# Host layouts for the streams, output and weights of a two-layer diffusion block, and first modulations taken chunk by chunk

## The chip, the cores and the metric

The kernel runs on one core of one Trainium2 chip. The metric is the device time of one execution in microseconds (us), median of several runs. A profiled execution gives the trace. TensorE is called PE in the rows, its weight loads PEld, VectorE DVE, ScalarE ACT, GpSimd POOL, and SyncE's issue of transfers SPq.

## The reference

Two consecutive layers work on 256 latent tokens (x) and 256 context tokens (ctx), each of width 1024, in float32. Each layer is a half-step feed-forward block, a mixing block, and a second half-step feed-forward block; each is modulated by shift, scale and gate vectors that a matrix w_mod makes from a conditioning vector:

```python
def rms_norm(x, gain=None):
    y = xf * lax.rsqrt(jnp.mean(xf * xf, axis=-1, keepdims=True) + EPS)
...
def modulate(h, shift, scale):
    return h * (1.0 + scale) + shift

def swiglu(h, w_gate, w_up, w_down):
    return (jax.nn.silu(h @ w_gate) * (h @ w_up)) @ w_down
```

The mixing of the even layer is windowed attention beside differential attention, that of the odd layer latent attention beside neighbourhood attention. Nine modulation vectors a layer are silu(c) @ w_mod + b_mod, once for the latent tokens (from c) and once for the context tokens (from c_ctx). Only the latent tokens are returned.

## The kernel before

**Layout.** The stream lies transposed in SBUF as `xT`: eight chunks k of 128 features by 512 tokens (latent 0 to 255, context 256 to 511). A weight block of 512 KB (four k-chunks of 128 rows by 256 columns) is loaded by `wcols` (L269) into one of three buffers `raw`; in a (1024, 2816) matrix that is 512 pieces of 1 KB. `split` then writes two reduced-precision halves into `hs`: high on ACT (L99), low on DVE (L100). Each product is three matmuls, high by high, high by low, low by high, in `mm3` (L103).

**A feed-forward block.** For each pair of 128-column groups, `gps0, gps1` (gate) and `ups0, ups1` (up) are summed over the eight chunks of `hT`, the modulated and normed stream; then ACT makes silu (`sg`, L428), DVE the product (`af`), both are split (`ah`), and later `dps` (down) goes back into `xT` (L295).

**The start.** The tokens are loaded as they come, 128 tokens by 1024 features (`xin`, L505). ACT squares and sums them (L549); PE transposes them in 32 pieces (`xps`, L555), and ACT and DVE copy these into `xT`. c, c_ctx and b_mod are loaded as rows and transposed too (`cps`, `bps`). The first feed-forward block needs shift and scale of layer 0, 1024 values each for two streams, from 8 MB of w_mod: in four quarters q of two chunks each. `first_loads(q)` issues four loads of 512 KB (`wm`, L515), `first_mods(q)` runs 32 small matmuls into `mps` (L524; each is two records in the trace), copies it (`mst`, L527), transposes (`mpt`, L529) and adds the bias (L96), and `first_norm(q)` makes `xn` (L540) and `hT` (high L542, low L543). For the first pair of the first block the product is interleaved with the quarters: as soon as chunks 0 and 1 of `hT` are there, their 24 matmuls can run.

**The other modulations** are not matmuls: rows of the transposed w_mod (`mraw`, L202, 512 KB each) are multiplied by `cb` (c and c_ctx broadcast to all partitions, L199, silu in place at L200) and summed by one DVE instruction for each (L212). This stream of parts is called between the matmuls (`pump_every`), from the first pair on.

**The end.** The last block computes the latent tokens alone. For each of the eight chunks of the result `emit_out` transposes two halves (`otp`, L488), copies them into `ot` (L491 on ACT, L493 on DVE), and writes 128 by 256 values after every second chunk (L496).

**Order.** A scheduler of the language places every instruction in its engine's list before the run; each engine then works through its own list in order, and semaphores join the lists. All large transfers are issued by SP, in order. A transfer waits at SP for its buffer to be free and for the semaphore of the transfer that stood eight places earlier; those behind it wait with it.

Of the kernel before, what the change touches and what calls it, by code (L numbers as in the profile page):

```python
# [16 lines left out]
P = 128  # L17
# [23 lines left out]
UNITS = {"kq": 15, "ot": 6, "pr": 9, "pt": 10, "w2": 8, "wm": 16, "xn": 4, "hT": 8, "raw": 3, "hs": 5, "mraw": 3}  # L41
# [22 lines left out]
def tile_hybrid_dit(ctx: ExitStack, tc: tile.TileContext, I, out, dbg=None):  # L64
# [101 lines left out]
    bT = const("bT", [P, 2, 9, KC])  # L166
    brow = w2("brow")[:72, :256]
    Q.dma_start(out=brow.rearrange("n (l p) -> n l p", l=2), in_=I["b_mod"].rearrange("l (n p) -> n l p", p=P))

    S.activation(cvec, cvec, AF.Silu)  # L170
    cps = bank("tr", "cps")
    T.transpose(cps[:, :16], cvec, ident[:16, :16])
    for v in range(2):
        V.tensor_copy(cT[:, :, v], cps[:, 8 * v:8 * v + 8])
    bps = bank("tr", "bps")
    for l in range(2):
        T.transpose(bps[:, 72 * l:72 * l + 72], brow[:, l * P:(l + 1) * P], ident[:72, :72])
    V.tensor_copy(bT, bps[:, :144].rearrange("p (l m k) -> p l m k", l=2, m=9))
# [86 lines left out]
    def wcols(w, k0, nk, c0, nw, tag=None):  # L265
        n = nk * nw
        src = w[k0 * P:(k0 + nk) * P, c0:c0 + nw].rearrange("(k p) f -> p k f", p=P)
# [14 lines left out]
    xall = xp.tile([P, KC, NTOK], F32, tag="xT", name="xT")  # L282
    xT = [xall[:, k, :] for k in range(KC)]
# [197 lines left out]
    outs = {}  # L481

    def emit_out(dc):
        if dc % 4 == 0:
            outs["t"] = [w2(f"ot{b}") for b in range(2)]
        for b in range(2):
            pt = bank("tr", "otp")
            T.transpose(pt[:, :P], xT[dc][:, b * P:(b + 1) * P], ident)  # L488
            o = outs["t"][b][:, (dc % 4) * P:(dc % 4 + 1) * P]
            if b:  # L490
                S.copy(o, pt[:, :P])  # L491
            else:
                V.tensor_copy(o, pt[:, :P])  # L493
            if dc % 2 == 1:
                c0 = (dc % 4 - 1) * P
                Q.dma_start(out=out[b * P:(b + 1) * P, (dc - 1) * P:(dc + 1) * P],  # L496
                            in_=outs["t"][b][:, c0:c0 + 256])


    ss0 = const("ss0", [P, 4])  # L500
    xin = []
    for tb in range(4):
        t = up.tile([P, D], F32, tag="kq", name=f"xin{tb}", bufs=UNITS["kq"])
        src = I["x"][0] if tb < 2 else I["ctx"][0]
        Q.dma_start(out=t, in_=src[(tb % 2) * P:(tb % 2 + 1) * P, :])  # L505
        xin.append(t)


    def first_loads(q):
        tiles = {}  # L510
        for k0 in (0, 4):
            for m in (1, 0):
                t = up.tile([P, 4, 256], F32, tag="wm", name="wm", bufs=UNITS["wm"])
                c0 = m * D + 256 * q
                Q.dma_start(out=t, in_=I["w_mod"][0, k0 * P:(k0 + 4) * P, c0:c0 + 256].rearrange("(k p) f -> p k f", p=P))  # L515
                tiles[m, k0] = t
        return tiles

    def first_mods(q, tiles):
        ps = bank(("po", "md")[q % 2], "mps")  # L520
        for k in range(KC):
            for c in range(4):
# [8 lines left out]
        for m in (1, 0):  # L531
            for v in range(2):
                add(modT[:, 0, v, m, 2 * q:2 * q + 2], pv[:, 1 - m, :, v], bT[:, 0, m, 2 * q:2 * q + 2])
# [33 lines left out]
    def first_step(q):  # L567
# [3 lines left out]
        if q == 3:  # L571
            mod_done.update({(0, 1), (0, 0)})
# [769 lines left out]
```

## Time and profile before

| | us |
|---|---|
| median of 3 runs | 1815.4 (1815.14 to 1818.62) |
| the profiled execution, its time | 1815.71 |
| its span, first to last instruction | 1813.6 |
| PE busy | 1762.3 (97%) |
| DVE busy | 1220.6 (67%) |
| ACT busy | 738.8 (41%) |
| moved by transfers | 256.90 MB, mean 142 GB/s |

The span is what the rows below are set in; 2.1 us lie around it. A busy share of PE near the whole means that time can be won only where PE stands idle, runs slowly or does work that can go.

### The profile page before, as it was taken

The page shows a single profiled execution, that of the slowest core. Times are in us where ns is not written, and L with a number is a line of the kernel's source. Part 1 is how long each engine was busy: PE and PEld are TensorE (multiplying, and loading weights), DVE is VectorE, ACT ScalarE, POOL GpSimd, SP SyncE. Part 2 cuts the span into 40 slices and gives each one's busy share as a digit, 9 for nine tenths or more (in the row PEclk, how much of TensorE's full clock was granted, in tenths as well). Part 3 has the DMA queues.
Part 4 walks back from the last instruction along what each step waited for, and adds up shares of the span by engine and source line. Part 5 has one row for each costly group of instructions (what it writes and reads, how often), then busy time and mean ns, then how long its engine had stood idle before and what let it go on. Part 6 is the DMA issues. An engine that isn't in the chain of part 4 may idle for free.

```text
span 1813.6 us, 26777 instructions
## 1 busy us (share of the span) xinstructions
PE 1762.3 (97%) x10563; PEld 1537.5 (85%) x10563; DVE 1220.6 (67%) x2343; ACT 738.8 (41%) x1322; POOL 46.0 (3%) x25
## 2 busy tenths in 40 slices
PE   7999999999999989999999999999999998999999
PEld 5788888898998888888888988888889986789998
DVE  5999953467688699989854633333346787876664
ACT  4333132345666543222233332222334656664442
POOL 0000000011010000000000000000001011000000
PEclk9999999999999989999999999999999999999999
DMA  9777752322110237778863233233233442155552
GB/s 305 273 245 225 236 190 88 116 73 68 50 60 14 59 121 240 241 229 261 300 199 105 81 94 94 92 105 103 88 111 101 89 102 57 47 178 183 175 186 82
DMA packets 214025, 256.90 MB, mean 142 GB/s; under 512 B 21484, under 2 KB 195724, under 8 KB 213900
## 3 DMA queue, kind: packets, MB, share of 16 engines
q1 hardware_dynamic: 213900, 255.19, 45.6%
q8 instruction: 83, 1.36, 0.3%
q14 instruction: 42, 0.34, 0.1%
HBM read 254.11 MB, written 1.05 MB: 141 GB/s over the span
## 4 chain that ended last, share of the span: by engine, by line
PE 87%; DVE 7%; ACT 3%; DMA 2%; issue 1%; SPq 0%; DVEq 0%; ACTq 0%
PE ups L103 23%; PE gps L103 23%; PE dps L103 23%; PE ops L103 3%; PE po L756 2%; PE sc L103 2%; DVE hs L100 1%; DMA bias<-in_d_rpb_dram 1%; PE trp L659 1%; PE pbk L103 1%; PE pbv L103 1%; PE paq L103 1%; PE pbq L103 1%; PE ptl L724 1%; PE mps L524 1%
## 5 line engine op out<-in xcount | busy, mean ns | idle before, releaser
L100 DVE TENSOR_TENSOR hs<-raw,hs 128x1024 fp32r<-128x1024 f32 (+2 forms) x308 | 367.9, 1200 | 284.1 <-ACT hs L99 283.4
L99 ACT ACTIVATE hs<-raw 128x1024 fp32r<-128x1024 f32 (+2 forms) x308 | 314.9, 1030 | 541.4 <-PE dps L103 177.8
L103 PE MATMUL dps<-ah,hs 128*128 128x512 f32 (+1 forms) x2256 | 401.0, 338 | 0.2 <-DVE hs L100 0.2
L103 PEld LDWEIGHTS dps<-ah,hs 128*128 128x128 f32 x2256 | 350.6, 190 | 46.4 <-DVE hs L100 0.4
L103 PE MATMUL gps<-hT,hs 128*128 128x512 f32 (+1 forms) x1680 | 375.3, 380 | 4.9 <-ACT hT L542 2.7
L103 PE MATMUL ups<-hT,hs 128*128 128x512 f32 (+1 forms) x1680 | 371.6, 377 | 0.0
L103 PEld LDWEIGHTS gps<-hT,hs 128*128 128x128 f32 x1680 | 305.0, 190 | 65.5 <-ACT hT L542 3.5
L103 PEld LDWEIGHTS ups<-hT,hs 128*128 128x128 f32 x1680 | 303.3, 188 | 58.8 <-issue 1.0
L212 DVE CUSTOM_DVE_ANT_0 junk<-mraw,cb,const 128x1024 f32<-128x1024 f32 x224 | 283.6, 1283 | 16.3 <-DMA mraw<-in_k_w_modT_dram 11.1
L99 ACT ACTIVATE ah<-af 128x512 fp32r<-128x512 f32 (+1 forms) x88 | 50.4, 574 | 127.5 <-DVE af L93 93.9
L295 DVE SCALAR_TENSOR_TENSOR xT<-dps,const,xT 128x256 f32<-128x256 f32 x112 | 50.3, 480 | 77.0 <-PE dps L103 76.9
L276 POOL TENSOR_TENSOR hs<-raw,hs 128x1024 fp32r<-128x1024 f32 (+2 forms) x21 | 45.8, 2186 | 1558.2 <-ACT hs L275 1493.8
L93 DVE TENSOR_TENSOR af<-sg,ups 128x512 f32<-128x512 f32 x66 | 45.2, 685 | 41.0 <-PE ups L103 40.9
L103 PE MATMUL gps<-hTl,hs 128*128 128x258 f32 x528 | 66.8, 284 | 1.6 <-DVE hTl L373 1.0
L428 ACT ACTIVATE sg<-gps 128x512 f32<-128x512 f32 x66 | 38.9, 589 | 70.2 <-PE gps L103 70.2
L103 PEld LDWEIGHTS gps<-hTl,hs 128*128 128x128 f32 x528 | 64.7, 190 | 2.5 <-DVE hTl L373 1.2
L103 PE MATMUL ups<-hTl,hs 128*128 128x258 f32 x528 | 65.5, 283 | 0.0
L103 PEld LDWEIGHTS ups<-hTl,hs 128*128 128x128 f32 x528 | 64.4, 190 | 0.0
L100 DVE TENSOR_TENSOR ah<-af,ah 128x512 fp32r<-128x512 f32 (+1 forms) x88 | 54.6, 621 | 13.2 <-ACT ah L99 13.2
L684 DVE TENSOR_REDUCE nm<-sc 128x1 f32<-128x512 f32 (+1 forms) x80 | 53.8, 682 | 5.0 <-PE sc L103 4.6
L690 ACT ACTIVATE pr<-sc,nm 128x512 f32<-128x512 f32 (+1 forms) x64 | 40.3, 634 | 13.7 <-DVE nm L684 13.4
L304 ACT ACTIVATE sq<-xT 128x256 f32<-128x256 f32 (+1 forms) x54 | 23.6, 449 | 50.9 <-DVE xT L295 50.6
(296 smaller groups left out, 1894.3 us busy)
## 6 DMA issues: line engine op xcount, KB each, us to landing
mraw<-in_k_w_modT_dram SPq DMA_DIRECT2D x128, 512.0 KB, 4.6
raw<-in_ffn_w_gate_dram SPq DMA_DIRECT2D x88, 512.0 KB, 4.7
raw<-in_ffn_w_up_dram SPq DMA_DIRECT2D x88, 512.0 KB, 4.5
raw<-in_ffn_w_down_dram SPq DMA_DIRECT2D x80, 512.0 KB, 4.1
raw<-in_cd_w_in_dram SPq DMA_DIRECT2D x18, 512.0 KB, 3.8
wm<-in_w_mod_dram SPq DMA_DIRECT2D x16, 512.0 KB, 8.7
raw<-in_ab_w_in_dram SPq DMA_DIRECT2D x16, 512.0 KB, 3.8
raw<-in_ffn_w_down_dram SPq DMA_DIRECT2D x16, 256.0 KB, 2.7
```

Of the source, the lines that this page charges most:

```text
L93: V.tensor_tensor(out=out_, in0=a, in1=b, op=ALU.mult)
L99: S.activation(h, src, AF.Copy)
L100: V.tensor_tensor(out=l, in0=src, in1=h.bitcast(F32), op=ALU.subtract)
L103: T.matmul(ps, a, b, start=start, stop=stop)
L212: V.tensor_tensor_reduce(out=junk, in0=raw, in1=mod_c[v], scale=0.5 if m in (2, 8) else 1.0, scalar=bT[:, l, m, k:k + 1], op0=ALU.mult, op ...
L276: nc.gpsimd.tensor_tensor(out=hs[:, 1, :n], in0=raw[:, :n], in1=hs[:, 0, :n].bitcast(F32), op=ALU.subtract)
L295: V.scalar_tensor_tensor(out=xT[dc][:, a:e], in0=ps[:, a:e], scalar=modT[:, l, v, m, dc:dc + 1], in1=xT[dc][:, a:e], op0=ALU.mult, op1=ALU ...
L304: S.activation(sq[:, cols], xT[dc][:, cols], AF.Square)
L428: S.activation(sg, g[:, :ntok], AF.Silu)
L684: V.tensor_reduce(out=nm[:, c], in_=view, axis=AX.X, op=ALU.max, negate=True)
L690: S.activation(p[:, cols], sc[:, cols], AF.Exp, bias=nm[:, i + b:i + b + 1], accum_out=den[:, i + b:i + b + 1])
L756: T.matmul(po[64 * x:64 * x + 64, q], val(x, c), pts[x][c], start=c == order[0], stop=c == order[-1], tile_position=(0, 64 * x))
```

## The change

Weights of both feed-forward blocks, of the even layer's two mixing matrices and of the odd layer's output matrix are handed over in blocks, so that one `wcols` load is 128 pieces of 4 KB, one a partition. `cd_w_in`, `c_w_uq` and `c_w_ukv` stay as they were, and `mraw` had 4 KB pieces already. Tokens, c, c_ctx and b_mod come in transposed, so the 32 `xps` transposes, `cps`, `bps` and their copies go; the squares are now taken of `xT` chunk by chunk on ACT, summed by seven DVE additions, and summed over partitions by four matmuls `st0`. The output is written transposed straight from `xT`; the 16 `otp` transposes and their copies go. The first modulations come in five steps of 1, 1, 2, 2 and 2 chunks; a step of one chunk splits its sum over k in two halves that DVE joins (`mh`). Their loads go into four tiles of 16 KB a partition and are issued ahead in order.

```diff
-    cvec = w2("cvec")[:16, :P]
-    Q.dma_start(out=cvec[0:8], in_=I["c"].rearrange("o (k p) -> (o k) p", p=P))
-    Q.dma_start(out=cvec[8:16], in_=I["c_ctx"].rearrange("(k p) -> k p", p=P))
+    cvec = w2("cvec")[:, :2 * KC].rearrange("p (k v) -> p k v", v=2)
+    Q.dma_start(out=cvec, in_=I["k_cT"])
+    xall = xp.tile([P, KC, NTOK], F32, tag="xT", name="xT")
+    xT = [xall[:, k, :] for k in range(KC)]
+    for k in range(0, KC, 2):
+        Q.dma_start(out=xall[:, k:k + 2, :], in_=I["k_xT"][:, k:k + 2, :])
...
+        if len(w.shape) == 4:
+            assert nw == 256 and c0 % 256 == 0
+            src = w[c0 // 256, :, k0:k0 + nk, :]
+        else:
+            src = w[k0 * P:(k0 + nk) * P, c0:c0 + nw].rearrange("(k p) f -> p k f", p=P)
...
     def emit_out(dc):
-        if dc % 4 == 0:
-            outs["t"] = [w2(f"ot{b}") for b in range(2)]
-        for b in range(2):
-            pt = bank("tr", "otp")
-            T.transpose(pt[:, :P], xT[dc][:, b * P:(b + 1) * P], ident)
...
+        Q.dma_start(out=out[dc * P:(dc + 1) * P, :], in_=xT[dc][:, 0:256])
...
+    STEPS = ((0, 1), (1, 1), (2, 2), (4, 2), (6, 2))
+
+    wmall = [up.tile([P, 2, 2, D], F32, tag="wm", name="wm", bufs=4) for _ in range(4)]
...
+    def first_mods(j, nj, tiles):
+        ps = bank("po", "mps")
+        if nj == 1:
+            for k in range(4):
+                for c in range(4):
+                    T.matmul(ps[32 * c:32 * c + 32, :P], cT[:, k + 4 * (c % 2), :], tiles[1 - c // 2][k + 4 * (c % 2)],
+                             start=(k == 0), stop=(k == 3), tile_position=(0, 32 * c))
...
+    wms = [first_loads(*STEPS[0])]
+    for k in range(KC):
+        if k == 0:
+            S.activation(ssum, xT[k], AF.Square)
+        else:
+            xsq = w2("xsq")
+            S.activation(xsq, xT[k], AF.Square)
+            add(ssum, ssum, xsq)
+    st0 = bank("tr", "st0")
     for tb in range(4):
-        xsq = xall[:, 2 * tb:2 * tb + 2, :].rearrange("p k n -> p (k n)")
-        S.activation(xsq, xin[tb], AF.Square, accum_out=ss0[:, tb:tb + 1])
+        mm(st0[:, tb:tb + 1], ssum[:, tb * P:(tb + 1) * P], ones[:, 0:1], True, True)
...
+    bcs = bank("md", "bcs")
+    for b in range(4):
+        dg = small.tile([P, P], F32, tag="dg", name="dg", bufs=2)
+        V.tensor_scalar(out=dg, in0=ident, scalar1=rs0[:, b:b + 1], scalar2=None, op0=ALU.mult)
+        mm(bcs[:, b * P:(b + 1) * P], ones, dg, True, True)
...
+    def first_steps(b):
+        if b == 0:
+            wms[1:] = [first_loads(*step) for step in STEPS[1:]]
+        for i in ((1, 2), (3, 4))[b]:
+            first_mods(*STEPS[i], wms[i])
+            first_norm(*STEPS[i])
```

Three places show how the change stands in the engines' lists. The first is SP's list between the loads of the first modulations and the first weights of pair 1 (`raw_559`; before, `raw_601`): before, then after.

```order
L269 DMA raw_404<-in_ffn1_w_up_dram 128x4x256
L515 DMA wm_409<-in_w_mod_dram 128x4x256
L515 DMA wm_411<-in_w_mod_dram 128x4x256
L515 DMA wm_413<-in_w_mod_dram 128x4x256
L515 DMA wm_415<-in_w_mod_dram 128x4x256
L199 DMA cb_476<-in_c_dram 128x1024
L202 DMA mraw_482<-in_k_w_modT_dram 128x1024
L199 DMA cb_479<-in_c_ctx_dram 128x1024
L202 DMA mraw_532<-in_k_w_modT_dram 128x1024
L269 DMA raw_601<-in_ffn1_w_gate_dram 128x4x256
```

```order
L496 DMA wm_97<-in_k_wm0_dram 128x1024 x4
L265 DMA raw_310<-in_k_ffn1_w_gate_dram 128x1024
L265 DMA raw_315<-in_k_ffn1_w_up_dram 128x1024
L191 DMA cb_434<-in_c_dram 128x1024
L191 DMA cb_437<-in_c_ctx_dram 128x1024
L194 DMA mraw_440<-in_k_w_modT_dram 128x1024
L194 DMA mraw_490<-in_k_w_modT_dram 128x1024
L265 DMA raw_559<-in_k_ffn1_w_gate_dram 128x1024
```

Before, the semaphore that `cb_476` waits on is raised by the last matmul of quarter 2 (`mps_344`), one quarter ahead of the last. After, `cb_434` waits for the last matmul of the last step (`mps_375`), and everything below it waits with it.

The second is DVE's list from the last step's copy `mst` to the low half of pair 1's first weights (`hs_561`; before, `hs_603`): before, then after. The ISA rows with two names on the right are the modulation parts of L212 (L204 after).

```order
L540 SCALAR_TENSOR_TENSOR xn_465<-xT_99,const_79,bcs_183 128x256
L212 ISA junk_534,const_79<-mraw_482,cb_476,const_79 128x1024
L212 ISA const_79 128x1
L543 SCALAR_TENSOR_TENSOR hT_207<-xn_465,const_79,hT_207 128x256
L212 ISA junk_534,const_79<-mraw_482,cb_479,const_79 128x1024
L212 ISA const_79 128x1
L212 ISA junk_625,const_79<-mraw_532,cb_476,const_79 128x1024
L212 ISA const_79 128x1
L93 TENSOR_TENSOR af_586<-sg_585,ups0_474 128x512
L93 TENSOR_TENSOR af_593<-sg_592,ups1_475 128x512
L100 TENSOR_TENSOR hs_603<-raw_601,hs_603 128x1024
```

```order
L535 SCALAR_TENSOR_TENSOR hT_162<-xn_423,const_79,hT_162 128x256 x2
L204 ISA junk_492,const_79<-mraw_440,cb_434,const_79 128x1024
L204 ISA const_79 128x1
L204 ISA junk_492,const_79<-mraw_440,cb_437,const_79 128x1024
L204 ISA const_79 128x1
L204 ISA junk_583,const_79<-mraw_490,cb_434,const_79 128x1024
L204 ISA const_79 128x1
L204 ISA junk_583,const_79<-mraw_490,cb_437,const_79 128x1024
L204 ISA const_79 128x1
L100 TENSOR_TENSOR hs_561<-raw_559,hs_561 128x1024
```

Four modulation parts stand ahead of pair 1's first weights where three stood; the two products `af` moved behind them.

The third is the end of PE's list: before, then after.

```order
L103 MATMUL dps0_16985<-ah_16661,hs_16982 128x256 x3
L103 MATMUL dps0_16985<-ah_16675,hs_16982 128x256 x3
L103 MATMUL dps1_16986<-ah_16661,hs_16982 128x256 x3
L103 MATMUL dps1_16986<-ah_16675,hs_16982 128x256 x3
L488 MATMUL otp_17048<-const_79,xT_99 128x128
L488 MATMUL otp_17051<-const_79,xT_99 128x128
L488 MATMUL otp_17055<-const_79,xT_99 128x128
L488 MATMUL otp_17059<-const_79,xT_99 128x128
```

```order
L103 MATMUL dps0_16903<-ah_16619,hs_16900 128x256 x3
L103 MATMUL dps0_16903<-ah_16633,hs_16900 128x256 x3
L103 MATMUL dps1_16904<-ah_16619,hs_16900 128x256 x3
L103 MATMUL dps1_16904<-ah_16633,hs_16900 128x256 x3
L1355 UNCONDITIONAL_BRANCH
```

The list now ends with the last product. The other twelve `otp` stood between `dps` products of the same 240 and are gone too. Between the first 280 and the last 200 entries PE's list is the same in both programs.

## Rows read from the trace of the kernel before

**Rows 1.** The page's busy times of the engines, their share of the span and their instructions.

```profile
PE 1762.3 (97%) x10563; PEld 1537.5 (85%) x10563; DVE 1220.6 (67%) x2343; ACT 738.8 (41%) x1322; POOL 46.0 (3%) x25
```

**Rows 2.** Waits of PE over the whole span: what waited for what, us in total, how often, the longest. The first wait, at the start, and those in the mixing stages are left out.

```profile
PE gps L103 <- ACT hT L542: 2.7, 2, 1.8
PE gps L103 <- DVE hs L100: 1.3, 2, 1.1
...
PE otp L488 <- DVE xT L295: 0.5, 2, 0.3
```

**Rows 3.** The page's transfers: operation, count, KB each, median us from issue to landing.

```profile
mraw<-in_k_w_modT_dram SPq DMA_DIRECT2D x128, 512.0 KB, 4.6
raw<-in_ffn_w_gate_dram SPq DMA_DIRECT2D x88, 512.0 KB, 4.7
```

**Rows 4.** Windows: stretch and length, busy time (count) of PE, PEld, DVE, ACT, POOL, granted clock, DMA share, GB/s.

```profile
10.00:15.00 5.00, 5.00 (x24) 4.18 (x24) 3.12 (x16) 2.56 (x6) 0.00 (x0) 1.00 0.85 273
22.00:30.00 8.00, 7.27 (x79) 4.58 (x81) 4.78 (x9) 2.54 (x5) 0.00 (x0) 1.00 1.10 349
427.68:431.09 3.41, 3.18 (x15) 3.21 (x16) 1.27 (x4) 2.22 (x5) 0.00 (x0) 0.50 0.25 90
431.09:434.50 3.41, 3.41 (x31) 3.41 (x30) 0.61 (x4) 2.91 (x7) 0.00 (x0) 1.00 0.02 5
```

**Rows 5.** The chain that ended last, the first 75 us: start, us, what (PE pieces with their count).

```profile
10.44 2.56 PE xps L555 x12
...
17.52 0.44 PE xps L555 x4
...
22.73 1.38 PE gps L103 x4
24.10 0.34 PE mps L524 x4
...
25.57 1.00 PE mps L524 x28
...
47.65 1.00 PE mps L524 x28
...
59.35 10.27 PE gps L103 x44
69.62 10.88 PE ups L103 x48
```

**Rows 6.** Timeline of the start: start, us, engine, line, operation, output and input, count, idle time before it and its releaser.

```profile
11.10 1.06 ACT L549 ACTIVATE xT<-xin 128x1024 f32<-128x1024 f32 x1 [0.74 <-DMA xin<-in_ctx_dram]
...
12.15 0.57 ACT L559 COPY xT<-xps 128x512 f32<-128x512 f32 x1
12.25 0.69 DVE L557 COPY xT<-xps 128x512 f32<-128x512 f32 x1 [1.16 <-ACT xT L549]
...
12.86 0.16 DVE L113 TENSOR_SCALAR xe<-const 128x4 f32<-128x4 f32 x1
...
15.64 0.16 DVE L121 SCALAR_TENSOR_TENSOR const<-nt,const 128x4 f32<-128x4 f32 x1
15.84 0.48 DVE L323 TENSOR_SCALAR dg<-const 128x128 f32<-128x128 f32 x2
...
20.26 0.29 DVE L527 COPY mst<-mps 128x128 f32<-128x128 f32 x1 [0.19 <-PE mps L524]
...
24.02 1.22 DVE L100 TENSOR_TENSOR hs<-raw,hs 128x1024 fp32r<-128x1024 f32 x1
```

**Rows 7.** Timeline of the same kind, four matmuls `nst` of the shape that `st0` has, at a later norm.

```profile
385.32 0.58 PE L103 MATMUL nst<-const 128*128 128x1 f32 x4
```

**Rows 8.** Timeline again, from the first broadcast load to the low half of pair 1's first weights.

```profile
37.72 0.34 SPq L199 DMA_DIRECT2D cb<-in_c_dram  x1
...
51.73 1.04 ACT L200 ACTIVATE cb<-cb 128x1024 f32<-128x1024 f32 x1
...
54.33 1.29 DVE L212 CUSTOM_DVE_ANT_0 junk<-mraw,cb,const 128x1024 f32<-128x1024 f32 x1
...
55.54 1.29 DVE L212 CUSTOM_DVE_ANT_0 junk<-mraw,cb,const 128x1024 f32<-128x1024 f32 x1
...
58.08 1.22 DVE L100 TENSOR_TENSOR hs<-raw,hs 128x1024 fp32r<-128x1024 f32 x1
```

**Rows 9.** The tile `cb`: time from issue to landing of its six loads.

```profile
DMA to landing us min/median/max: 5.9/6.1/6.3
```

**Rows 10.** The chain that ended last, in the middle: the one wait for a weight of a changed layout.

```profile
477.19 3.89 DMA raw<-in_ab_w_in_dram
```

**Rows 11.** The chain that ended last, its last 36 us.

```profile
1778.03 6.48 PE dps L103 x54
...
1784.93 1.23 DVE hs L100
...
1802.15 7.19 PE dps L103 x60
...
1809.36 0.50 DVE xT L295
...
1809.90 0.45 PE otp L488 x2
```

**Rows 12.** Timeline of SP at the very end: the last two transfers, start of the first and end of the second issue.

```profile
1810.59 0.81 SPq L496 DMA_DIRECT2D out_dram<-ot  x2
```

More of the change, by code (lines that the diff above doesn't have):

```diff
@@ L165, in tile_hybrid_dit @@
     modT = const("modT", [P, 2, 2, 9, KC])
[L166 to L178, printed above, removed]
+    bT = const("bT", [P, 2, 9, KC], I["k_bT"])
+    S.activation(cT[:, :, 0:2], cvec, AF.Silu)
     for m0 in (1, 2):
@@ L500, in tile_hybrid_dit @@
[L500 to L516, printed above, removed]
-        return tiles
@@ L519, in first_mods @@
[L519 to L522, printed above, removed]
-                m, x = 1 - c // 2, c % 2
-                T.matmul(ps[32 * c:32 * c + 32, :P], cT[:, k, :], tiles[m, k - k % 4][:, k % 4, P * x:P * x + P],
-                         start=(k == 0), stop=(k == KC - 1), tile_position=(0, 32 * c))
+        Q.dma_start(out=out[dc * P:(dc + 1) * P, :], in_=xT[dc][:, 0:256])
+    STEPS = ((0, 1), (1, 1), (2, 2), (4, 2), (6, 2))
@@ new lines, in first_mods @@
+    def first_mods(j, nj, tiles):
+        ps = bank("po", "mps")
+        if nj == 1:
+            for k in range(4):
[4 more added lines that the diff above has]
+            for k in range(KC):
+                for c in range(4):
+                    x = c % 2
+                    T.matmul(ps[32 * c:32 * c + 32, :P], cT[:, k, :], tiles[1 - c // 2][k][:, P * x:P * x + P],
+                             start=(k == 0), stop=(k == KC - 1), tile_position=(0, 32 * c))
@@ L531, in first_mods, with first_norm @@
         for m in (1, 0):
-            for v in range(2):
-                add(modT[:, 0, v, m, 2 * q:2 * q + 2], pv[:, 1 - m, :, v], bT[:, 0, m, 2 * q:2 * q + 2])
-    def first_norm(q):
-        for k in range(2 * q, 2 * q + 2):
+            if nj == 1:
+                half = sml(2, "mh")
+                V.tensor_scalar(out=half, in0=pv[:, 1 - m, 0, 0:2], scalar1=bT[:, 0, m, j:j + 1], scalar2=None, op0=ALU.add)
+                add(modT[:, 0, :, m, j], pv[:, 1 - m, 1, 0:2], half)
+            else:
+                for v in range(2):
+                    add(modT[:, 0, v, m, j:j + 2], pv[:, 1 - m, :, v], bT[:, 0, m, j:j + 2])
+    def first_norm(j, nj):
+        for k in range(j, j + nj):
             t = unit("xn", "xn")
@@ L810, in mix0 @@
     def mix0():
[L811 removed]
+        w_in, w_out = I["k_ab_w_in"][0], I["k_ab_w_out"][0]
         tabs = {}
@@ L1319, in consts, with laid_out, blocks @@
     return c
-_OUT = (SEQ, D)
+_OUT = (D, SEQ)
+def laid_out(a):
+    import numpy as np
+    a = {k: np.asarray(v) for k, v in a.items()}
+    def blocks(w):
+        n, k, f = w.shape
+        return w.reshape(n, k // P, P, f // 256, 256).transpose(0, 3, 2, 1, 4)
+    c = {"k_xT": np.concatenate([a["x"][0], a["ctx"][0]]).T.reshape(KC, P, NTOK).transpose(1, 0, 2),
+         "k_cT": np.stack([a["c"][0], a["c_ctx"]]).reshape(2, KC, P).transpose(2, 1, 0),
+         "k_bT": a["b_mod"].reshape(2, 9, KC, P).transpose(3, 0, 1, 2),
+         "k_wm1": a["w_mod"][0, :, :2 * D].reshape(KC, P, 2, KC, P)[:, :, :, :2].transpose(3, 2, 1, 0, 4),
+         "k_wm0": a["w_mod"][0, :, :2 * D].reshape(KC, P, 2, 4, 256).transpose(3, 2, 1, 0, 4)}
+    for nm in ("ab_w_in", "ab_w_out", "cd_w_out", *(f"ffn{n}_w_{x}" for n in (1, 2) for x in ("gate", "up", "down"))):
+        c["k_" + nm] = blocks(a[nm])
+    return c
 def kernel(**inputs):
```

74 lines of the change are left out of this document (29 added, 45 removed).

## The prediction

> **What bounds the kernel now.** I read the busy times first: PE works in 1762.3 of 1813.6 us [rows 1], so time can come only from the places where PE waits or does work that goes. The waits of PE name no weight load in the feed-forward blocks: there they are for `hT` (2.7 us, all at the start), for the low halves `hs` (1.3 us) and for `xT` (0.5 us) [rows 2]. Where a weight load does appear is in the chain that ended last, once, 3.89 us at 477 us, before the first mixing matrix [rows 10]. Everywhere else loads of 512 KB, 4.6 to 4.7 us long [rows 3], land well before PE comes to them. So the change is worth what it does in the first 60 us and in the last 36 us, and I cost those two stretches instruction by instruction. The measure of PE's speed is 48 matmuls of 512 columns in 10.88 us, 0.2267 us each [rows 5].
>
> For the start I need one mark: pair 1 begins its run without gaps at 59.35 us with 44 of its 48 gate matmuls left [rows 5]; four of 0.2267 us were done before, so its equivalent start is 58.44 us.
>
> **The end.** From 1778.03 us on PE has 240 `dps` matmuls. The last 60 take 7.19 us without a gap [rows 11], so 240 take 28.76 us. Before, they lasted until 1802.15 + 7.19 = 1809.34 us, 31.31 us: 2.55 us are transposes and a wait in which DVE reached `hs` (1784.93, 1.23 us) only after `xT`. After, no transpose stands between them, and PE takes the blocks in order, so that 7.19 us of products cover each 1.23 us of `hs`: the wait goes as well. Then the exit: the last `xT` ends at 1809.36 + 0.50 = 1809.86 us [rows 11]; before, two transposes and a copy followed, and the last two issues began at 1810.59 and took 0.81 us together, so the last began near 1811.0 [rows 12]. After, it begins right behind `xT`, near 1809.9: 1.1 us less, the piece written being the same 128 by 256 values. Together **-3.65 us**. Bounds: -4.0, if the step to the last transfer is a little shorter still, and -2.5, if a wait for `hs` of about 1.2 us stays.
>
> **The middle.** The 3.89 us wait [rows 10] is a load issued late; the only row that tells 4 KB pieces from 1 KB pieces at equal size is `mraw`, 4.6 us, against the gate weights, 4.7 [rows 3]. I take **-0.2 us** (bounds -0.4 and 0). All other faster loads cost and bring nothing, since PE waits for none of them.
>
> **The start, to the first gate matmul (G).** Before, G is 22.73 us [rows 5]. After, it hangs on the last chunk of `xT`. The last token load let its square start at 11.10 us [rows 6]; the same 2 MB now stand right behind one small load, and I put its landing at 10.3 us (9.9 to 11.1). Behind it come two squares at 0.57 and an addition at 0.69, priced as the 128 by 512 copies [rows 6]: 1.83 us. Four matmuls `st0` as four `nst`, 0.58 [rows 7]. The twelve small steps of the inverse root, from 12.86 to 15.80 with one copy of 0.69 between: 2.25 us; four `dg` at 0.24: 0.96 [rows 6]; the last broadcast and `mps` matmuls, 0.5 (estimate from PE's rows). From the copy `mst` (20.26) to G (22.73) 2.47 us, as before [rows 5, 6]; but DVE's list now has the low half of the first weights in this path: 1.22 us [rows 6]. Eight handovers between engines at about 0.2 us, the idle time before `mst` [rows 6]: 1.6 us. Sum 11.4, G = 21.7; bounds 20.7 to 23.3.
>
> **From G to the end of the last step's matmuls (T0).** PE's list has 48 product matmuls there, 10.88 us, and 220 small `mps` records. A block of 28 takes 1.00 us and one of 4 takes 0.34 [rows 5], which is 0.0275 a record and 0.23 a block; with another 0.2 us when PE turns back to products I take 0.45 a block. After has 12 blocks: 5.4 + 6.0 = 11.4 us. With the last transpose 22.6 us (21.8 to 24). The loads keep up: 11.5 MB up to there, at 349 GB/s [rows 4], have landed near 36 us, and T0 is 21.7 + 22.6 = 44.3.
>
> **From T0 to pair 1.** This is where the change adds a wait. `cb` is now issued after T0; behind it at SP stand the second `cb`, two `mraw` and pair 1's first weights. Before, it went out at 37.72 [rows 8], before the last quarter was done. A `cb` load lands 6.1 us after its issue [rows 9], T0 + 6.2. ACT makes its silu, 1.04 us [rows 8], half of the last `hT`, the second silu and the other half (0.5 each), T0 + 9.3; DVE makes the last low half, T0 + 9.8, then the four parts, 1.21 us apart (54.33, 55.54), T0 + 14.7, then the low half of pair 1's weights, 1.22 [rows 8]: T0 + 15.9. Two matmuls of each three need only the high half, so the equivalent start is T0 + 15.4 (14.8 to 16.4). PE itself would have been ready sooner: its 48 remaining products, 10.88 us, begin with high halves soon after T0 and wait some 2 us for `hs`, T0 + 13.5. Pair 1 starts at 44.3 + 15.4 = 59.7 us: **+1.3 us**.
>
> **The clock.** The first twelve transposes took 2.56 us, 0.213 each, and the last four 0.44, 0.11 each [rows 5]: PE worked at half rate until near 15 us, though the granted clock column shows 1.00 for 10 to 15 us [rows 4]. Before, those 5 us fell on transposes, while the loads were still under way. After, PE has only some 3 us of scattered work ahead of G, and the half rate may fall on the first products. Bounds: 0, if it rises as early as before; 2.5 us, if 5 us at half rate come after G. Later in the run a stretch at 0.50 (1.2 GHz) lasted 3.41 us with PE busy 3.18, and the next showed 1.00 [rows 4], which would cost 1.6. Part is hidden where PE waits for `hT`. I take **+1.0 us**.
> The Trainium skill ("TensorE: Matmul & The Clock Gate", Part 4: PE-mode transpose) says that transposes do not bring up the full clock, as they do not count as work for it; then their loss costs nothing here, and the sum would be 1813.2. The trace speaks against it for these transposes: 24 records fill 10 to 15 us, nearly all of them transposes, and the next ones run at the full rate.
>
> **Sum.** -3.65 - 0.2 + 1.3 + 1.0 = -1.55 us against the profiled execution's 1815.71: 1814.2 us. That execution lies 0.3 us above the median of the runs shown, well inside their spread. About 0.2%, 3.6 us, is what a measurement of this kernel can tell from no change: below 1811.8 it is faster, above 1819.0 slower. The terms at the end add to nearly that bound, and the start decides how much of them is kept.
>
> **Rivals.**
> *The start costs nothing.* G at its early bound 20.7, the way to T0 21.8, T0 + 14.8, no loss by the clock: pair 1 at 57.3, -1.1 us. With the terms at the end -5.0, 1810.8 us; with half of these gains about 1811.6. For it: fewer PE instructions at the start, one step of 1 MB ahead of G instead of a quarter of 2 MB. Against it: the longer chain of small DVE steps behind the last chunk, and `cb` behind T0. It takes in the case in which the Trainium skill's rule on transposes holds.
> *The start eats the end.* G 23.3, 24 us to T0, T0 + 16.4, or the whole 2.5 us of the clock with some of these: +3 to +6 us, 1815.5 to 1818.5 us. The mechanism is that the change does not do what it says: the first loads do not wait on each other, but `cb` waits on the last of their matmuls and takes the next pair's weights with it.
> *Slower: PE at half rate until T0.* Each product then costs another 0.2267 us, 48 of them 10.9 us: -3.65 - 0.2 + 1.3 + 10.9 = +8.4, 1824 us. It decides against the kernel from about 6 us of full-rate work done at half rate, some 12 us of stretch. For it: PE has small blocks with gaps there. Against it: from 22 to 30 us PE was busy for 7.27 of 8 us with the same mixture [rows 4], at its full rate, and the stretch at 0.50 in the middle ended after 3.4 us.
>
> **How the numbers follow.** The forecast, 1812 to 1815.5, has a chance of 0.47; the start that costs nothing, 1810.2 to 1811.8, 0.30; the start that eats the end, 1815.5 to 1819, 0.15; the slower case 0.08. Faster by over 0.2% is then 0.30, within it 0.62, slower 0.08. The range 1810.2 to 1817.5 leaves out the slower case and the worse half of the third.
>
> **What the changed profile would show.** The end: `dps` from its first to its last in 28.8 us, no gap, and the last issue within 0.1 us of the last `xT`. The start: the first gate matmul near 21.7, the last `mps` near 44, `cb` issued right behind it, its two silus before the four parts of L204, and pair 1 without gaps from about 60 us. The clock: the first products after G at 0.43 us or 0.23 each. In between each stage as long as before. I am wrong if pair 1 starts before 58 or after 63 us, or if the middle moves by more than 1 us, which would mean that the layout of the weights reaches PE by a way that I do not see.

## The result, and the profile after

The changed kernel takes 1839.8 us (median of 4 runs, 1837.38 to 1840.73) against 1815.39 of the kernel before beside it: ratio 1.0128, 95% interval 1.0111 to 1.0146. It is 24 us slower; the forecast was 1814.2, with 1810.2 to 1817.5 as range. The profiled execution spans 1838.2 us against 1813.6.

The page's first lines. PE has 42 instructions less than in [rows 1] and is busy 18.3 us longer:

```profile
span 1838.2 us, 26666 instructions
PE 1780.6 (97%) x10521; PEld 1536.9 (84%) x10521; DVE 1223.5 (67%) x2338; ACT 735.1 (40%) x1309; POOL 45.9 (2%) x25
```

So most of the time did not come from waiting. I set PE's records of the two traces against each other, matmul by matmul; each difference in the table is what a stretch gained in length.

| stretch of the kernel before, us | longer by, us |
|---|---|
| start to pair 1 | +5.3 |
| first, second, third block of 512 tokens | +6.5, +6.7, +6.5 |
| even layer's mixing | -2.2 |
| odd layer's mixing, 1385 to 1476 | +5.4 |
| its rest (+0.6), and between the blocks (-0.6) | 0.0 |
| the end | -3.5 |
| sum | +24.7 |

**The end** went as forecast. The chain that ended last has 240 `dps` without a gap, where [rows 11] had transposes and a wait:

```profile
1806.18 28.61 PE dps L103 x240
1834.79 0.02 issue
1834.82 0.48 DVE xT L289
```

**The blocks** did not. In the same view, the first groups behind pair 1; [rows 5] had 10.88 us for each 48:

```profile
74.81 11.20 PE ups L103 x48
86.00 11.05 PE gps L103 x48
97.06 11.20 PE ups L103 x48
```

No row shows a wait there. The matmuls of such a group simply start 0.230 to 0.233 us after one another, on average, instead of 0.227. The next two lines are the changed kernel's 512-column gate and up products, grouped by shape (busy time in us, mean ns of one); the kernel before has 346.5, 390 and 345.4, 390 in them:

```profile
L103 PE MATMUL gps<-hT,hs 128*128 128x512 f32 x1488 | 354.5, 396 | 4.1 <-ACT hT L534 2.7 <-DVE hs L100 1.4
L103 PE MATMUL ups<-hT,hs 128*128 128x512 f32 x1488 | 354.2, 395 | 0.0
```

The 512-column down products of the same blocks grow likewise (263.5 to 268.7 us). Products of 256 columns do not.

**The start.** The chain of the changed kernel, from the sums of squares to pair 1 (G and T0 are the forecast's marks: the first gate matmul, and the end of the last step's matmuls):

```profile
11.92 1.88 PE st L103 x8
...
16.63 1.19 PE bcs L103 x4
...
24.07 1.22 PE gps L103 x2
25.29 1.85 PE mps L505 x28
...
34.28 1.00 PE mps L511 x28
...
47.70 1.02 PE mps L511 x28
48.74 0.30 DVE mst L514
...
51.78 1.21 PE gps L103 x2
...
63.76 6.38 PE gps L103 x28
```

The same 28 small records take 1.85 us at 25.29 and 1.00 at 34.28: PE worked at half rate until near 28 us, where the kernel before had its full rate from near 15 [rows 5]. After T0 (48.7) the chain waits three us for DVE and ACT, and then the granted clock falls. Windows (stretch, length, busy PE, PEld, DVE, ACT, POOL, granted clock, DMA share, GB/s):

```profile
20.00:25.00 5.00, 2.13 (x10) 0.87 (x7) 4.23 (x11) 0.91 (x2) 0.00 (x0) 1.00 1.03 417
51.70:55.20 3.50, 3.42 (x8) 2.77 (x9) 3.22 (x7) 2.53 (x4) 0.00 (x0) 0.52 1.01 405
55.20:58.60 3.40, 3.40 (x16) 2.75 (x16) 2.67 (x4) 1.18 (x3) 0.00 (x0) 0.99 1.03 419
```

**The odd layer's mixing.** Its bias tables (`bias`, L1048; L1053 before, eight transfers for two heads) are issued by SP between weight loads. The second such set in the chain, before:

```profile
1434.34 0.63 SPq L1053
1435.02 10.39 DMA bias<-in_d_rpb_dram
1445.60 0.69 DVE bias L96
```

and after, where the mixing itself began 22.2 us later, so that 1462.83 stands 5.6 us later in its stage than 1435.02:

```profile
1462.03 0.76 SPq L1048
1462.83 10.41 DMA bias<-in_d_rpb_dram
1473.32 0.69 DVE bias L96
```

PE also loses its clock in these waits: the granted clock of the changed kernel shows 0.50 from 1461.5 and from 1478.6 us, for 3.4 us each, and its matmuls fall up to 28.8 us behind those of the kernel before. But the chain runs through DVE and ACT there. Where it comes back to PE (`trp` at 1484.19, before at 1456.65) the lag is 27.5 us, no more than that of the landing of the bias (1473.24 against 1445.41, 27.8). So by this chain the half rate did not lengthen the stage.

### The profile page after: what moved, and what is told of

It is laid out like the page before. It is cut to its first block, busy times and chain, and to the rows that moved or that the text cites. A ratio compares the mean times of both kernels' runs of the same rounds, so it can differ in the third digit from the quotient of the medians.

```text
span 1838.2 us, 26666 instructions
## 1 busy us (share of the span) xinstructions
PE 1780.6 (97%) x10521; PEld 1536.9 (84%) x10521; DVE 1223.5 (67%) x2338; ACT 735.1 (40%) x1309; POOL 45.9 (2%) x25
## 4 chain that ended last, share of the span: by engine, by line
PE 86%; DVE 7%; ACT 3%; DMA 2%; issue 1%; SPq 1%; DVEq 0%
PE ups L103 24%; PE gps L103 23%; PE dps L103 23%; PE ops L103 2%; PE po L751 2%; PE sc L103 2%; DMA bias<-in_d_rpb_dram 1%; DVE hs L100 1%; PE paq L103 1%; PE trp L654 1%; PE pbk L103 1%; DVE const L96 1%; PE pbq L103 1%; PE pbv L103 1%; PE bpo L103 1%
## 5 line engine op out<-in xcount | busy, mean ns | idle before, releaser
L103 PE MATMUL gps<-hT,hs 128*128 128x512 f32 (+1 forms) x1680 | 383.3, 385 | 5.2 <-ACT hT L534 2.7
L103 PE MATMUL ups<-hT,hs 128*128 128x512 f32 (+1 forms) x1680 | 380.1, 382 | 0.0
L204 DVE CUSTOM_DVE_ANT_0 junk<-mraw,cb,const 128x1024 f32<-128x1024 f32 x224 | 283.3, 1281 | 14.9 <-DMA mraw<-in_k_w_modT_dram 11.7
```

Source lines behind the costliest of these rows:

```text
L103: T.matmul(ps, a, b, start=start, stop=stop)
L204: V.tensor_tensor_reduce(out=junk, in0=raw, in1=mod_c[v], scale=0.5 if m in (2, 8) else 1.0, scalar=bT[:, l, m, k:k + 1], op0=ALU.mult, op ...
```

## The experiments

Ratios are to runs of the kernel before made beside each kernel on the same chip. Where a stage is said to have grown, it is by the same setting of PE's records against the kernel before.

**What slowed the matmuls.** The built programs say where tiles lie in a partition of SBUF. `const` is 14,544 bytes, 16 past a multiple of 64, and what lies behind it starts 32 past one. Before, all of `hs` (weights) and `hT` (moving operand) lay behind `const`. After, the four `wm` tiles of 16 KB lie ahead of it, and four of the five places of `hs` take over their room, at multiples of 64. In some three quarters of the gate and up products the operands then differ by 32 bytes modulo 64.

Theory: this difference costs the 20 us. Rivals: the absolute place counts, or something in transfers of 4 KB. Three kernels tell them apart: the changed one with `const` padded, so that all places of `hs` and `hT` are multiples of 64 (e1); the kernel before with the same padding (e2); and the kernel before with the weights' new layout alone (e3: `wcols` and the host's blocks, as in the diff of the change).

```diff
-NCONST = 3636
+NCONST = 3648
```

> The changed kernel with its tile of constants 48 bytes longer (NCONST 3648 for 3636), so that every tile behind it starts 32 bytes later; before that, four of five weight buffers hs began at a multiple of 64 bytes and the moving operand hT 32 bytes past one; now both begin at multiples of 64. Theory 'phase' (a 512-column matmul takes 0.227 us where weights and moving operand stand at the same place modulo 64 bytes, 0.232 to 0.235 where not): all matmuls of the three 512-token blocks at 0.227, 20 us less than the changed kernel, 1818 to 1822 us. Rival 'transfers' (pieces of 4 KB, at up to 419 GB/s, slow PE's reads): no change, 1838 to 1841 us. Rival 'absolute' (weights that begin at a multiple of 64 are slow by themselves): 1839 to 1845 us.

> The kernel before with the same 48 bytes added: hs and hT both move from 32 bytes past a multiple of 64 to a multiple of 64, together. 'Phase': no change, 1814 to 1817 us. 'Absolute': all matmuls of 512 columns 5 to 8 ns longer, 1838 to 1842 us. 'Transfers': no change.

> The kernel before with the weight layouts alone (4 KB a piece), everything else and all addresses as before. 'Phase': matmuls stay at 0.227 us, 1814 to 1816 us (0 to 0.5 us less than before, at the one wait of 3.9 us for a weight). 'Transfers': matmuls at 0.232, 1831 to 1838 us.

Measured: the padded changed kernel 1820.38 us, ratio 1.0020 (1.0010 to 1.0029), 19 us less than unpadded. Its chain:

```profile
74.45 10.88 PE ups L103 x48
85.33 10.88 PE gps L103 x48
96.22 10.88 PE ups L103 x48
```

The kernel before, padded: 1816.77, ratio 0.9996 (0.9987 to 1.0006). With 4 KB pieces alone: 1816.29, ratio 1.0000 (0.9991 to 1.0010). The absolute place and the pieces are out; the relation of the two operands stays. To bring it into the kernel before, its 16 `wm` tiles were cut out of four of 16 KB (d1):

```diff
+        whole = up.tile([P, 2, 2, 4, 256], F32, tag="wm", name="wm", bufs=4)
...
-                t = up.tile([P, 4, 256], F32, tag="wm", name="wm", bufs=UNITS["wm"])
+                t = whole[:, k0 // 4, m]
```

> The kernel before; the only edit is that the first modulations' 16 weight tiles of 4 KB are cut out of four tiles of 16 KB. Nothing else in the program's work changes: same loads, same order, same matmuls, quarters as before. In the built program the pieces of hs then stand at 49792 and 57984 (a multiple of 64) and at three places that are 32 past one, and hT stays 32 past one, so about two of every five weight loads stand otherwise to 64 bytes than the moving operand does. Theory (a 512-column matmul whose weights and moving columns differ modulo 64 bytes takes some 233 ns instead of 227): the rows of 48 matmuls of the 512-token blocks rise from 10.88 to a mixture of 10.88 and about 11.1 to 11.2 us, the three blocks grow by about 2 to 3.5 us each, and the whole by 6 to 10 us, ratio 1.0033 to 1.0055; nothing grows at the start or the end. Rival (what made the three blocks of the changed kernel longer is something else in its start, such as its loads or its order, and the padding of const undid it by chance): the time stays within 2 us of that of the kernel before, ratio 0.999 to 1.001.

Measured: 1831.17, ratio 1.0071 (1.0055 to 1.0087), which is 13 us and more than expected. The three blocks grew by 3.6, 3.1 and 3.5 us, at the upper edge of what was expected, and show both kinds of group in one program, as two of five places of `hs` are moved:

```profile
72.27 11.20 PE ups L103 x48
83.47 10.88 PE gps L103 x48
94.35 11.04 PE ups L103 x48
```

Setting each record against the addresses in its program gives the time from one 512-column start to the next: in this kernel 227.7 ns where both operands stand 32 past a multiple of 64 (2532 pairs) and 233.3 where the weights stand at a multiple and the moving operand 32 past (1571); in the changed kernel 227 (700, median) and 233.4 (2248). The other way round, in the 59 products of `ah` that have it, it is 233.8. Beyond the blocks its profiled execution loses 4.2 us in the odd layer's mixing, which I come to, and 2.6 at the start, of which the even layer's mixing gives back 2.3.

The start of one and the same program differs by that much between executions, and the execution of the kernel before that is shown here was an early one. Of nine profiled executions of other kernels that keep its start (four of them with the 4 KB pieces), one (`mraw` 2, below) comes to pair 1 0.3 us earlier; eight come 0.5 to 2.0 us later, each with a granted clock of 0.50 for 3.4 us somewhere between 22.4 and 27.7 us, where the one shown had 1.00. In the kernel before with the padding (windows, columns as above):

```profile
23.10:26.50 3.40, 3.40 (x11) 1.86 (x10) 3.40 (x6) 1.25 (x2) 0.00 (x0) 0.50 1.10 352
```

**The end alone**, in the kernel before (`emit_out` as in the change, e4), and then with the 4 KB pieces (f4):

> The kernel before with the new exit alone (output written transposed from xT, no otp, no copies). My step for the end says -3.65 us (2.55 within the last 240 products, 1.1 behind them): 1811.5 to 1812.5 us. A rival that the wait for hs in the last stage stays: -2.5 us, 1813 us.

> The kernel before with the pieces of 4 KB and the output written transposed from xT, nothing else. Theory (the two add, 0 and -3): 0.9975 to 0.999 of the kernel before, rows of 48 at 10.88 us. Rival (the other layout moves places in SBUF or the order at SP): the end still shorter by 3 us, but a stage in the middle longer by 3 us or more, ratio 0.9995 to 1.002.

Measured: 1814.1, ratio 0.9985 (0.9975 to 0.9995), 3.0 us by the medians; with the pieces 1813.37 against 1816.85, ratio 0.9979 (0.9969 to 0.9988). The end is worth what was forecast, and the second kernel is faster than both the kernel before and the changed one.

**The clock at the start.** The padded changed kernel with 50 small matmuls on `ones` in gaps of PE's start (e5; the ten others are not shown):

```diff
+    hot = bank("sc", "hot")
+    for i in range(40):
+        mm(hot[:, :P], ones, ones, True, True)
```

> e1 (the changed kernel with the 48 bytes) plus 50 matmuls of ones by ones into a spare bank, 40 ahead of the first st0 and 10 in PE's gaps before the first gate matmul; nothing reads them. Theory 'clock': the 5.2 us that the start loses are half-rate work (st0 8 records 1.88 us, bcs and mps 4.0 us, the first 28 mps 1.85 us, and a stretch at 0.50 from 51.8 us on); with PE busy from the start the first gate matmul comes near 21 us in place of 23.9 and pair 1 near 59 to 60 in place of 63.6: 4 to 5 us less than e1, 1815.5 to 1816.5 us. Rival 'chain' (the start is lost to the longer list of small DVE steps and to cb behind the last step): within 1 us of e1, 1819.5 to 1821 us.

Measured: 1816.84, ratio 1.0003 (0.9993 to 1.0013), 3 us under the padded kernel by the two ratios. Pair 1 comes 1.1 us after that of the kernel before instead of 4.8, about as late as in most executions with the old start. In its chain the `st` and `mps` pieces take half of what they took above, and one fall of the clock is left, again behind the wait after T0:

```profile
13.09 0.79 PE st L103 x8
...
22.25 0.73 PE gps L103 x2
22.98 1.00 PE mps L505 x28
```

```profile
48.00:51.40 3.40, 3.40 (x8) 2.72 (x9) 3.06 (x6) 2.61 (x4) 0.00 (x0) 0.50 0.93 371
51.40:55.20 3.80, 3.80 (x18) 3.14 (x18) 3.12 (x6) 1.38 (x3) 0.00 (x0) 1.00 1.03 419
```

**What lengthened the odd layer's mixing.** The kernel asks for three `raw` buffers, but in the built program of the kernel before `raw` has a fourth place in this stage, which the changed one lacks. A load gets a `raw` place once the load that held it has been split. In the changed program the last weight load ahead of the first bias takes the place of the load three before it, in the kernel before that of four before; it goes out at 1442.40 us, 4.0 later in its stage than in the kernel before, and the bias loads behind it at SP go with it. The first try gave the changed kernel `wm` as 16 small tiles and `mraw` a fourth buffer, which was to give `raw` a fourth place (e6); the second took an `mraw` buffer from the kernel before, which takes the fourth place from its `raw` (e7):

```diff
-"raw": 3, "hs": 5, "mraw": 3}
+"raw": 3, "hs": 5, "mraw": 2}
```

> The changed kernel with the first modulations' weights in 16 tiles of 4 KB a partition in place of 4 of 16 KB, and four mraw buffers in place of three. By the built program the tiles then stand as they stood before (hs and hT both 32 bytes past a multiple of 64), and the weight loads of the odd layer's mixing go round four places, as before, not three. Theory 'phase': matmuls at 0.227 without the 48 bytes, so that it was the 16 KB tiles that moved hs. Theory 'place': the 6.3 us that the odd layer's mixing loses (its bias loads are issued 4.7 us later, behind a weight load that waits for its place) come back: 6 us less than e1, 1813.5 to 1815 us. Rival (the bias loads are late for another reason): as e1, 1820 us.

> The kernel before with two mraw buffers for three; by the built program the weight loads of the odd layer's mixing then go round three places, where they went round four. Theory 'place': the first bias loads are issued 4 to 5 us later against the stage's start and the stage takes 5 to 6.5 us more, whatever the fewer buffers cost elsewhere. Rival: the stage is as long as before within 1 us.

Measured: the small tiles 1819.37, ratio 1.0021 (1.0012 to 1.0031). Groups of 48 were at 10.88 us without padding, as the addresses (both 32 past) ask for, but the mixing still grew by 4.4: `raw` had four places, and the last load ahead of the bias still took that of three before. So the number of places was the wrong quantity. The kernel before with its fourth place gone: 1821.7, ratio 1.0036 (1.0025 to 1.0048), its mixing 7.2 us longer, and SP with the wait of the changed kernel in it (timeline of SP: two weight loads over 4.63 us, then the bias):

```profile
1414.38 4.63 SPq L269 DMA_DIRECT2D raw<-in_cd_w_in_dram  x2
1419.06 6.15 SPq L1053 DMA_DIRECT2D bias<-in_d_rpb_dram  x8
```

The small tiles with the small matmuls as well (e8) were to add up both gains, and did not:

> e6 with the 50 matmuls of e5. If 'phase', 'place' and 'clock' are separate causes their gains add: e6 less 4 to 5 us, 1809 to 1811 us, 0.3 to 0.4% less than before. If the start is not the clock: as e6.

Measured: 1818.78, ratio 1.0014 (1.0004 to 1.0023). Pair 1 came 3.5 us late, as it did without the small matmuls. They did work: the first gate matmul came at 21.46 us instead of 24.05. But behind it the granted clock fell to 0.50 from 22.2 to 25.6 us, and then the chain waits twice for the loads of the 16 small tiles, which the padded kernel with its four tiles of 16 KB does not:

```profile
30.05 7.21 DMA wm<-in_k_wm_dram
...
38.65 6.85 DMA wm<-in_k_wm_dram
```

So in this kernel the loads decide when pair 1 starts. Why PE lost the clock at 22.2 us with the same matmuls in front is not settled.

Then I took the bias loads off SP, to ACT's queue, in the kernel before (d4) and in the padded kernel with the small matmuls (d2):

```diff
-                    Q.dma_start(out=bias[r:r + 64, c0:c0 + 256].rearrange("p (j k) -> p j k", j=4), in_=src)
+                    S.dma_start(out=bias[r:r + 64, c0:c0 + 256].rearrange("p (j k) -> p j k", j=4), in_=src)
```

> The kernel before with the bias loads of the odd layer issued from ACT's queue alone. Theory (the loads stand at SP behind weight loads, in the kernel before too): the first scores wait less, and the mixing of the odd layer becomes 2 to 8 us shorter, time 1808 to 1814, ratio 0.9955 to 0.999. Rival (before, the place of the raw buffers was not late, so that nothing is to be won): within 1.5 us of the kernel before; or 1 to 4 us slower if ACT's issues hold up its other work.

> The changed kernel with const padded to a multiple of 64 bytes and the 50 small matmuls at the start (as in e5_after_pad_warm); the only further edit is that the bias tables of the odd layer are loaded from ACT's queue and not from SP's, where they stand behind weight loads that wait for a raw place. Theory (the 6 us that the odd layer's mixing grew by are bias loads late behind a weight load at SP): the stretch from the first sc to the end of that mixing loses at least those 6 us, so 6 to 10 us under e5_after_pad_warm, time 1807 to 1811, ratio to the kernel before 0.995 to 0.9975. Rival (the growth is contention of the bias transfers themselves, 10.4 us each for pieces of 4 bytes in another order, or ACT, which then issues, is held up by it): the time stays within 2 us of e5_after_pad_warm, about 1817, or rises by up to 3 us.

Measured: 1846.23, ratio 1.0157 (1.0140 to 1.0174), and 1842.93, ratio 1.0134 (1.0114 to 1.0153); a third, the kernel before with the faster end and the pieces (d3), came to 1839.9, ratio 1.0130, where 0.994 to 0.9975 was expected. All are misses; by the ratios each is 24 to 29 us slower than the same kernel with the loads at SP. ACT works through its own list, so the loads go out only when ACT comes to them, and nothing has been fetched ahead. The chain of the kernel before with this edit waits for one set after the other, between them only DVE's and ACT's work on the last:

```profile
1424.35 7.19 DMA bias<-in_d_rpb_dram
...
1435.10 5.16 DMA bias<-in_d_rpb_dram
...
1445.55 7.15 DMA bias<-in_d_rpb_dram
```

These say that the stage hangs on the bias loads, but nothing of the late place. So I moved them ahead in SP's own order, the first two heads' in front of three weight loads (`bias_loads` split from `score`, called as items `bd` of the order; f1 is the padded kernel with the small matmuls, f3 the kernel before with pieces and end):

```diff
-MIX1 = """dq00 cq00 g f dk00 dk01 sd0 sd2 dv00 dv01 cq20 rd0 sd1 sd3 ...
+MIX1 = """dq00 cq00 g f bd0 bd2 dk00 dk01 sd0 sd2 dv00 dv01 cq20 rd0 bd1 bd3 sd1 sd3 ...
```

> The changed kernel with const padded and the small matmuls at the start (as e5_after_pad_warm); the further edit is that the bias loads of the odd layer's neighbourhood heads are an item of their own, the first two heads' eight loads three weight loads earlier in SP's order, the others one item earlier. Theory (the stage grew because these loads stood behind a weight load whose raw place was late): the first bias issue comes some 20 us before the scores need it and not 4 us later than in the kernel before, and the odd layer's mixing loses the 6 us and perhaps some of the 10 that the kernel before waited there: 1804 to 1812 us, ratio to the kernel before 0.993 to 0.9975. Rival (the transfers themselves, 64-element rows in pieces of 4 bytes that take 7 to 11 us, contend with the weights, so that it does not matter when they start): within 2 us of e5_after_pad_warm, ratio 0.999 to 1.0015.

> The kernel before with three edits: weights in pieces of 4 KB, output written transposed from xT, and the bias loads ahead of the weight loads as in f1. Theory: -3 for the end, 0 for the pieces, and for the bias loads what the stage of the kernel before loses to them, 3 to 10 us: 1804 to 1811, ratio 0.993 to 0.9975. Rival (in the kernel before they come early enough, and what follows them bounds the stage): the end alone, -2 to -4 us, ratio 0.998 to 0.999.

(The pieces of a bias transfer are rows of 64 values, 256 bytes, not 4 as the expectations here and above put it.) Measured: 1817.97, ratio 1.0004 (0.9994 to 1.0014), and 1820.26, ratio 1.0016 (1.0005 to 1.0026), that is 7 us slower than the same kernel without the move. Both fall. The first set went out 20 us earlier in its stage than in the kernel before, but the six weight loads behind it then filled SP until 1435.7 in f1, and the second set, of heads 1 and 3, waited behind them as before (timeline of SP):

```profile
1395.02 6.39 SPq L1053 DMA_DIRECT2D bias<-in_d_rpb_dram  x8
1401.52 34.08 SPq L265 DMA_DIRECT2D raw<-in_cd_w_in_dram  x6
1435.68 6.12 SPq L1053 DMA_DIRECT2D bias<-in_d_rpb_dram  x8
```

It is the second set that the stage follows, to within 2 us. In the kernel before with `wm` in four tiles, whose weight load ahead of the first set was not late, SP waited, ahead of the second set, for the bias tiles' own places (waits of the queue: what waited for what, us in total, times, longest):

```profile
SPq L1054 <- DVE rd L698: 4.3, 2, 3.3
```

For each kernel: by how much its last issue came later in the stage than in the kernel before, and by how much the stage (1385 to 1476 us) grew, both in us.

| kernel | last issue of the second set | stage |
|---|---|---|
| before: padded; pieces; end; pieces and end | 0.0 in all | +0.7, -0.1, +0.7, +1.8 |
| changed, small tiles; the same with small matmuls | +4.1, +4.0 | +4.4, +4.1 |
| before, `wm` in four tiles | +4.6 | +4.2 |
| changed | +5.6 | +5.4 |
| changed, padded; the same with small matmuls | +5.8, +5.9 | +6.3, +6.2 |
| that, bias moved ahead | +6.9 | +6.5 |
| before with pieces and end, bias moved ahead | +8.3 | +6.3 |
| before, `mraw` 2 | +8.6 | +7.2 |

Last, the transfers left out, so that the scores lack their bias, in the padded kernel with the small matmuls (x1) and in the kernel before (x2):

```diff
-                    Q.dma_start(out=bias[r:r + 64, c0:c0 + 256].rearrange("p (j k) -> p j k", j=4), in_=src)
...
-                add(bv, bv, over(cmask.rearrange("p (o k) -> p o k", o=1), [P, 8, 64]))
+                add(bv, cm, cm)
```

> The changed kernel with const padded and the small matmuls at the start (as e5_after_pad_warm), without the transfers of the bias tables of the odd layer's neighbourhood heads: the mask is added to itself in their place, the same DVE instruction, so the scores lack their bias. Theory (the bias loads late at SP are the whole of the 6 us by which this stage is longer in the changed kernel): the stage loses what the kernel before loses in x2_before_nobias and 6 us besides, and from layer-1 scores to its outputs the two last equally long, within 1.5 us; the time is 3 to 5 us under that of x2_before_nobias (the end's 3.5, with the start and the even layer as in e5). Rival (weight loads with a late raw place hold PE by themselves): x1 stays about 1 to 3 us above x2_before_nobias, as e5 stands to the kernel before when the 6 us are in.

> The kernel before without the transfers of the bias tables, as x1 (the scores lack their bias). The chain of waits of the kernel before gives 10.39 and 7.08 us to these transfers and some 6 to SP's issues ahead of them, while PE has other work beside most of it. If this stage is bound by them in the kernel before too, it loses 4 to 12 us: 1804 to 1812, ratio 0.9935 to 0.998; if they are covered there, under 1.5 us.

Measured: 1811.29, ratio 0.9971 (0.9962 to 0.9981), and 1818.69, ratio 1.0012 (1.0002 to 1.0021). In the first the whole of the odd layer's mixing is as long as in the kernel before (-0.2 us), so the 6 us are gone with the transfers. The second did not become shorter, but 3.5 longer. Without the bias tiles its program too gives the last weight loads of this stretch the places of three loads before. Up to 1495 us the two kernels' stages agree within 0.3 us, and with that of the kernel before within 0.5, where the padded kernel with its transfers has 5.8 more. What parts them behind that is the clock. Matmul by matmul, the second loses 1.4, 0.9 and 1.0 us to the first in three stretches in which its granted clock shows 0.50; the first has no such stretch there (windows of the second, columns as above):

```profile
1501.90:1505.31 3.41, 3.41 (x15) 3.23 (x14) 2.59 (x6) 1.06 (x4) 0.00 (x0) 0.50 0.03 10
1518.96:1522.38 3.42, 3.42 (x12) 2.82 (x13) 2.31 (x6) 2.67 (x7) 0.00 (x0) 0.50 0.45 152
1573.58:1576.99 3.41, 3.41 (x13) 2.81 (x12) 2.87 (x6) 2.24 (x6) 0.00 (x0) 0.50 0.00 0
```

The expected equality within 1.5 us, and the 3 to 5 us between the times (7.4 measured), are a miss. So the 6 us of the changed kernel go with the bias transfers; that a late place costs something through the weights alone is not excluded.

## Why the prediction was wrong, step by step

**The middle, forecast -0.2: the step that failed, by 20 us.** It took PE's speed as given, 48 matmuls in 10.88 us, and asked only what PE waits for. The edit that mattered was a line I did not price at all, `wmall` in tiles of 16 KB: it changed where `hs` lies against `hT`. The forecast named the sign ("the middle moves by more than 1 us") and the wrong carrier: the weights' layout in DRAM is worth nothing (1.0000), their place in SBUF 19 us (1839.8 to 1820.4 by padding). The wait of [rows 10] is gone from the chain, and the even layer's mixing 2.2 us shorter; but the kernel before with the new end alone, whose mixing is untouched, shows -2.2 there too, so the -0.2 is neither shown nor refuted.

**The odd layer's mixing, forecast 0: failed, +5.4.** "PE waits for none of them" was read from PE's waits. The weight loads reach PE by another way: a load that waits at SP for its place holds the bias loads behind it, and these hold the scores.

**The start, forecast +2.3 with the clock, measured +5.3.** G was to come at 21.7 and came at 24.07. The work ahead of it was sized well (the squares and additions end at 11.88, against 12.1); what was missed is the half rate: `st` 1.88 us for 0.58, two times `bcs` at 1.19 and 1.15 instead of 0.64. G to T0 took 24.7 for 22.6. T0 to pair 1 took 15.0 for 15.4, and that for another reason: PE does not wait for `cb`, whose two loads landed in 4.2 and 5.1 us and not 6.1. It waits three us for the last `hT` and `hs`, then runs its 48 products, some at half rate. The term that was mis-sized is the clock, +1.0 (0 to 2.5): in the padded kernel the small matmuls alone took 3.7 us off the start. With them G came at 22.25, G to T0 took 22.7 and T0 to pair 1 14.9, so pair 1 stood at 59.82, where the sum without the clock has 59.7. These are single executions, and about 1 us of the +5.3 is the early execution of the kernel before. The rival in which PE runs at half rate until T0 did not come: the full rate was there from 28 us.
The Trainium skill's rule on transposes ("TensorE: Matmul & The Clock Gate", Part 4), weighed in the forecast, gets no support here: with the transposes gone the full rate came 13 us later, and matmuls in their room brought it back.

**The end, forecast -3.65: right.** -3.5 in the changed kernel, -3.0 alone (interval -4.5 to -0.9).

With the failed steps mended and the start as measured the sum is -3.5 - 2.2 + 5.3 + 19.7 + 5.4 = +24.7. Of these, padding gives back 19, small matmuls 3; what stays, 6 us of the odd layer, eats the end. Two figures of the rivals do not follow from their terms: +3 to +6 us at the start gives 1814.9 to 1817.9 and not 1815.5 to 1818.5, and no row gives the 1811.6; neither changes the judgement.

## What to carry to other kernels

When an edit changes a tile's size or count, compare the addresses of the matmul operands in the two built programs: a buffer of the start can move the weights of the whole run. A weight load that PE never waits for still costs if small loads that the next stage needs stand behind it on the same queue, so follow a late place down the queue. If every group of equal matmuls is a few per cent longer and no wait has grown, look at places and at the clock, not at the schedule.

## What the runs showed that I had not expected

- A matmul of 512 columns took 227 ns where weights and moving operand had the same place modulo 64 bytes (both 0 or both 32) and 233 where they differed by 32; with 256 columns it was 118 ns where they differed and 119 to 120 where not, so no longer. Sixty down products of the kernel before have the difference too, at 234. Only these two places were seen.
- The changed kernel's PE ran at half rate until near 28 us while the granted clock column shows 1.00 there; the durations of equal pieces tell it, not the column.
- Transfers of 4 KB pieces moved 405 to 419 GB/s in the start's full windows, where 1 KB pieces moved 349 [rows 4]; the kernel before did not become faster by it.
- The bias transfers, 64 KB each, took 4.6 to 10.8 us from issue to landing in the changed kernel (median 7.1), where its loads of 512 KB into `raw` have medians of 3.6 to 4.6.
